# Eight merge-gate tiles of the latent branch moved from attention fillers into the 2x2 block products, with a new fill rate for the latent attention

## The chip, the core and the metric

The kernel runs on one core of one Trainium2 chip. A core has TensorE (PE) for matmuls, which writes only to PSUM, VectorE (DVE), ScalarE (ACT) and GpSimd (POOL) for elementwise work, and SyncE (SP), which issues the transfers here. Each engine works through its own instructions in their written order; semaphores make it wait for the others. The metric is the device time of one execution in microseconds (us).

## The reference

One layer of a bidirectional encoder, sequence 1024, width 1024, all in float32. `h` is the normalised input; one combined projection gives the inputs of two attentions, two SiLU gates `z` and two sigmoid merge gates `g`.

```python
h = rmsnorm(x, attn_norm_g)
(c_q, c_kv, k_rope, z_mla, q_dil, k_dil, v_dil, z_dil,
 g_mla, g_dil) = jnp.split(h @ w_in, split_points, axis=-1)
a_out = mla_attention(c_q, c_kv, k_rope, ...)      # 8 heads, 1024 x 1024 scores each
y_mla = (a_out * jax.nn.silu(z_mla)) @ w_o_mla
d_out = dilated_mixture(q_dil, k_dil, v_dil, positions)   # 24 heads, dilations 1, 4, 16
y_dil = (d_out * jax.nn.silu(z_dil)) @ w_o_dil
gate_mla = jax.nn.sigmoid(g_mla + b_gate[:D_MODEL])
gate_dil = jax.nn.sigmoid(g_dil + b_gate[D_MODEL:])
return x + (gate_mla * y_mla + gate_dil * y_dil) @ w_out   # then a final rmsnorm
```

`g_mla` is 1024 channels wide: eight tiles of 128 channels. These eight tiles are what the change is about.

## The kernel before

Every product is made from float32 pairs: an operand is split into a high part (a copy on ScalarE) and a low part (a subtraction on VectorE or POOL), and three matmuls high x high, high x low, low x high are added up (`mm3`, lines 77 to 79; `split`, lines 83 and 84). One such step on 512 columns is three matmuls; a projection tile of 128 channels by 512 tokens has eight steps, so a whole tile of 1024 tokens has 16 steps or 48 matmuls.

The stages follow each other in the program: the latent inputs and the dilated values (to about 228 us of the trace); the **block stage**; the **dilated attention**; the **latent attention**; the **end** (output gates and the last projection).

In the block stage (`blocks`, `block_steps`) the queries and keys of the dilated attention are computed by a 2x2 block scheme with seven products in place of eight: an item is two weight tiles and both token halves, seven products of four steps, 84 matmuls where two plain tiles have 96. There are twelve items. The results lie in four PSUM tiles a, b, c, d (`st_a` and so on); VectorE and ScalarE add them up, rotate them, and the result goes through the tiles `dq_st` to DRAM (`s_dq`, `s_dk`). POOL makes four block differences and seven low parts per item.

All other tiles of the combined projection that are needed late are **fillers**: the generator `fillers` walks through the list `ZG`, one step at a time, and the attentions call `feed(n)` at fixed places; `feed` adds up fractions and takes one step for each whole one. After the list the generator loads the eight pieces of the dilated branch (line 599, `zg_z` and `zg_t`, two buffers each, result in `brd_h`, `brd_l`), goes through 64 steps of the projection `w_o_dil` and then 48 of `w_o_mla` (three of its four parts; the fourth needs the last heads and stays for the end). What of these 48 steps is left when the latent attention ends is computed in the stage `output`.

In the dilated attention the order is written out by hand, fillers included. Its last pair is finished by `combine`: the softmax statistics are transposed (line 1083), sent through DRAM (`s_sd`, `c_sn`), made into factors on VectorE (lines 1098 to 1121), sent through DRAM again (`s_rr`, `bc`), and multiplied in (line 1134). In the latent attention a scheduler sets the order; a filler step is tied to the scores or transposes before it. A unit there is two query blocks of 128 rows of one head: scores `s_mla`, row maxima (line 740), exponentials `p` (line 743), transposes `pt` in four groups through two PSUM buffers (line 754), their split, and value products `av` (lines 762, 763).

Of the kernel before, what the change touches and what calls it, by code (L numbers as in the profile page):

```python
# [10 lines left out]
F32 = mybir.dt.float32  # L11
F32R = mybir.dt.float32r
I32 = mybir.dt.int32
AF = mybir.ActivationFunctionType
ALU = mybir.AluOpType
# [14 lines left out]

FIRST_FEED = 19
DIL_FEED = (1.43, 1.43, 2.5, 2)
FEED = (0.95, 0.95)

NB_BC = 5
NB_A = 6
# [3 lines left out]
T_ZM, T_QK = 0, 24  # L40

LEAD = 5

ZG = (4, 5, 6, 7, 0, 1, 2, 3, *range(16, 24), *range(8, 16))


def run_all(gen):
# [7 lines left out]
class Net:  # L55
# [393 lines left out]
    def block_steps(self, n, item, ps, tp):  # L449

        nc = self.nc
        v, act = nc.vector, nc.scalar
        a, b, c, d = (ps[x] for x in "abcd")
# [6 lines left out]
        def both():  # L460
# [9 lines left out]
            7: [lambda: add(c, 2)],  # L470
            9: [lambda: add(d, 2)],
        }
        _, g, quad, which = item
        parts = 2 if g < 2 else 1
        dst = (self.dq if which == 0 else self.dk)[g][4 * quad:4 * quad + 4]
# [59 lines left out]
                    elif half:  # L535
                        self.dma(dst[j, i, :, 0], st[i, 0][x])

        put = lambda k, f: steps.setdefault(k, []).append(f)
        r0, r1 = rope(0, b, c), rope(1, d, a)
        put(7, r0[0])  # L540
        put(8, r0[1])
# [168 lines left out]
    def mla_attention(self, ap, pp):  # L710
        nc = self.nc
        v = nc.vector
        for pair in range(4):
# [3 lines left out]
            for hh in range(2):  # L717
# [10 lines left out]
                for u in range(4):  # L728
# [3 lines left out]
                    for b2 in range(2):  # L732
                        qb = u * 2 + b2
                        qs = slice(128 * qb, 128 * qb + 128)

                        s = self.sp2.tile([128, S], F32, name="s_mla")
                        for kb in range(2):
                            ks = slice(512 * kb, 512 * kb + 512)
                            self.anchor = self.mm3(s[:, ks], q[:, 0, qs], q[:, 1, qs], k[:, 0, ks], k[:, 1, ks], True, True)
                        v.tensor_reduce(out=nm[:, hh, qb:qb + 1], in_=s, axis=AX.X, op=ALU.max, negate=True)  # L740
                        self.feed(FEED[0])
                        p = self.p_first.pop() if self.p_first else self.bp.tile([128, S], F32, name="p", bufs=3)
                        nc.scalar.activation(out=p, in_=s, func=AF.Exp, bias=nm[:, hh, qb:qb + 1], accum_out=den[:, hh, qb:qb + 1])  # L743
                        P.append(p)
# [3 lines left out]
                    for cp in range(4):  # L748
                        pt = pp.tile([128, 512], F32, name="pt", bufs=NB_PT)
                        for c2 in range(2):  # L750
                            for b2 in range(2):
                                kc = cp * 2 + c2
                                o = c2 * 256 + b2 * 128
                                self.anchor = nc.tensor.transpose(pt[:, o:o + 128], P[b2][:, 128 * kc:128 * kc + 128], self.ident)  # L754
                        self.feed(FEED[1])
                        ph = ap.tile([128, 512], F32R, name="pt_h", bufs=2)
                        pl = ap.tile([128, 512], F32R, name="pt_l", bufs=2)
                        self.split(pt, ph, pl, v)
                        for c2 in range(2):
                            kc = cp * 2 + c2  # L760
                            s = slice(c2 * 256, c2 * 256 + 256)
                            nc.tensor.matmul(a_out, vv[:, kc], ph[:, s], start=kc == 0, stop=False)  # L762
                            nc.tensor.matmul(a_out, vv[:, kc], pl[:, s], start=False, stop=kc == 7)  # L763
# [468 lines left out]
    def run(self):  # L1232
        tc, nc = self.tc, self.nc
        with ExitStack() as ctx:
# [24 lines left out]
            with tc.tile_pool(name="wpx", reuse_waits="tile", bufs=2, side="right") as self.wpx, tc.tile_pool(name="cosd", reuse_waits="tile", bufs=1, side="right") as dpool, ExitStack() as sums:  # L1259
# [34 lines left out]
                        for p in range(2):  # L1294
                            self.dma(self.dk[0][:, :, :, p, r:r + 64].rearrange("h c x t -> (c x) h t"), z[:64])
                with tc.tile_pool(name="dt", reuse_waits="tile", bufs=1, side="right") as tp, tc.tile_pool(name="st", reuse_waits="tile", bufs=1, space=PSUM) as pp:
                    self.blocks([(T_QK + (g * 2 + quad) * 4 + which * 2, g, quad, which) for quad in range(2) for g in range(3) for which in range(2)], tp, pp)
            at = ExitStack()
            pp = ctx.enter_context(tc.tile_pool(name="at", reuse_waits="tile", bufs=1, space=PSUM))
            self.dil_done, self.mla_done, self.brm, self.early, self.stop = False, 0, None, [], False  # L1300
# [98 lines left out]
```

## Time and profile before

| | |
|---|---|
| three timed runs | 1281.53, 1284.01 (median), 1286.01 us |
| the profiled execution | span 1288.1 us; no other time is given for it, so the span stands for it |
| busy, whole span | PE 1236.5, DVE 752.6, ACT 609.2, POOL 506.7 us |
| chain that ended last | PE 69%, DMA 10%, issue 4%, DVE 3% |
| transfers | 219.43 MB, mean 170 GB/s |

How to read it: a matmul's row lasts longer than its share of TensorE, since one matmul begins while the one before still drains; what one costs is the distance from start to start. The share of busy time is a mean over stages that are limited by different things, so the prediction goes by stages. In rows of the timeline the numbers are start and duration in us, and in brackets the time that the engine stood idle before the row, with what ended it.

### The profile page before, as it was taken

What the parts mean: (1) busy time and instruction counts of PE and PEld (TensorE: products, weight loads), DVE (VectorE), ACT (ScalarE), POOL (GpSimd) and SP (SyncE); (2) the same over time, 40 slices, a digit from 0 to 9 for tenths busy, and PEclk for the clock granted to TensorE, in tenths of its full rate; (3) what the DMA queues carried; (4) which work ended last, traced back from release to release, by engine and by line L of the source; (5) the groups of instructions that cost most, each with busy time, mean ns of one, the idle gap of its engine ahead of it and who ended that gap; (6) DMA issues with size and microseconds to landing.
All of it is one profiled execution on the core that took longest, in us unless ns stands there. A gap on an engine that the chain in (4) does not pass through costs nothing.

```text
span 1288.1 us, 19688 instructions
## 1 busy us (share of the span) xinstructions
PE 1236.5 (96%) x6957; PEld 1073.3 (83%) x6957; DVE 752.6 (58%) x1368; ACT 609.2 (47%) x1276; POOL 506.7 (39%) x402
## 2 busy tenths in 40 slices
PE   8979999899999999999998999999999999998998
PEld 8978999788888877888887888888888888885786
DVE  7483524466556644566565664555566666668632
ACT  6523336344444326555464552455555555554322
POOL 2342218877767715435323041311211211247522
PEclk9989999999999998999998999999999999998999
DMA  9946674276456685988879797445346535135441
GB/s 328 251 157 251 237 286 143 85 181 160 129 140 155 146 218 153 212 197 221 207 202 235 185 229 190 155 118 134 127 115 172 143 97 150 58 107 184 159 148 49
DMA packets 134482, 219.43 MB, mean 170 GB/s; under 512 B 37160, under 2 KB 66672, under 8 KB 130480
## 3 DMA queue, kind: packets, MB, share of 16 engines
q1 hardware_dynamic: 134384, 218.17, 60.2%
q8 instruction: 55, 0.90, 0.3%
q14 instruction: 43, 0.35, 0.1%
HBM read 149.37 MB, written 68.75 MB: 169 GB/s over the span
## 4 chain that ended last, share of the span: by engine, by line
PE 69%; DMA 10%; issue 4%; DVE 3%; POOL 2%; SPq 2%; ACT 1%; DVEq 0%; POOLq 0%; ACTq 0%
PE pj L77 10%; PE pj L78 10%; PE pj L79 10%; PE pt L754 4%; PE av L763 2%; DMA op_a<-s_dk 2%; PE s_mla L77 2%; PE s_mla L79 2%; PE av L762 2%; PE s_mla L78 2%; DMA bc<-s_rr 2%; PE st_a L77 2%; PE st_a L79 2%; PE st_a L78 2%; PE st_c L79 2%
## 5 line engine op out<-in xcount | busy, mean ns | idle before, releaser
L84 POOL TENSOR_TENSOR w_l<-w_raw,w_h 128x512 fp32r<-128x512 f32 (+1 forms) x176 | 227.0, 1303 | 416.8 <-ACT w_h L83 360.2
L77 PE MATMUL pj<-hT_h,w_h 128*128 128x512 f32 x384 | 156.3, 407 | 0.0
L79 PE MATMUL pj<-hT_h,w_l 128*128 128x512 f32 x384 | 152.1, 396 | 0.0
L78 PE MATMUL pj<-hT_l,w_h 128*128 128x512 f32 x384 | 152.0, 396 | 0.0
L83 ACT CAST w_h<-w_raw 128x512 fp32r<-128x512 f32 (+1 forms) x176 | 104.3, 615 | 82.3 <-POOL w_raw L427 70.4
L84 DVE TENSOR_TENSOR pt_l<-pt,pt_h 128x512 fp32r<-128x512 f32 x128 | 88.0, 688 | 66.9 <-ACT pt_h L83 66.0
L83 ACT CAST pt_h<-pt 128x512 fp32r<-128x512 f32 x128 | 74.7, 585 | 79.7 <-PE pt L754 47.7
L77 PE MATMUL pj<-w_h,hT_h 128*128 128x256 f32 x384 | 109.2, 284 | 0.0
L78 PE MATMUL pj<-w_l,hT_h 128*128 128x256 f32 x384 | 109.0, 284 | 0.0
L79 PE MATMUL pj<-w_h,hT_l 128*128 128x256 f32 x384 | 108.9, 283 | 0.0
L740 DVE TENSOR_REDUCE m_nm<-s_mla 128x1 f32<-128x1024 f32 x64 | 78.2, 1222 | 27.0 <-PE s_mla L79 26.3
L870 DVE CUSTOM_DVE_ANT_0 p<-s_ps,masks 128x256 f32<-128x256 f32 x128 | 48.8, 419 | 73.6 <-PE s_ps L861 63.9
L877 ACT ACTIVATE p<-p,d_st 128x256 f32<-128x256 f32 x128 | 64.1, 502 | 54.3 <-DVE d_st L870 54.2
L79 PEld LDWEIGHTS pj<-hT_h,w_l 128*128 128x128 f32 x384 | 72.9, 190 | 15.8
L77 PEld LDWEIGHTS pj<-hT_h,w_h 128*128 128x128 f32 x384 | 73.4, 191 | 11.2
L78 PEld LDWEIGHTS pj<-hT_l,w_h 128*128 128x128 f32 x384 | 73.2, 191 | 11.3
L743 ACT ACTIVATE p<-s_mla,m_nm 128x1024 f32<-128x1024 f32 x64 | 71.8, 1122 | 18.6 <-PE pt L754 17.6
L754 PE MATMUL pt<-consts,p 128*128 128x128 f32 x512 | 78.1, 272 | 1.3 <-ACT p L743 1.3
L77 PEld LDWEIGHTS pj<-w_h,hT_h 128*128 128x128 f32 x384 | 73.7, 192 | 0.9
L78 PEld LDWEIGHTS pj<-w_l,hT_h 128*128 128x128 f32 x384 | 73.6, 192 | 0.8
L79 PEld LDWEIGHTS pj<-w_h,hT_l 128*128 128x128 f32 x384 | 73.7, 192 | 0.8
L762 PE MATMUL av<-pt_h,op_c 128*128 128x256 f32 x256 | 68.8, 289 | 0.0
(307 smaller groups left out, 3320.0 us busy)
## 6 DMA issues: line engine op xcount, KB each, us to landing
w_raw<-wt SPq DMA_DIRECT2D x48, 512.0 KB, 3.7
op_b<-s_dq SPq DMA_DIRECT2D x32, 512.0 KB, 8.4
gate<-s_gt SPq DMA_DIRECT2D x43, 256.0 KB, 2.9
s_dq<-dq_st SPq DMA_DIRECT2D x80, 128.0 KB, 2.4
s_dk<-dq_st SPq DMA_DIRECT2D x80, 128.0 KB, 2.4
s_dv<-dv_st SPq DMA_DIRECT2D x32, 256.0 KB, 4.1
s_gt<-zg_t SPq DMA_DIRECT2D x32, 256.0 KB, 3.7
w_raw<-wv SPq DMA_DIRECT2D x12, 512.0 KB, 3.6
```

The source lines that it names most:

```text
L77: mm(out, lh, rh, start=start, stop=False, skip_group_check=skip)
L78: mm(out, lh, rl, start=False, stop=False, skip_group_check=skip)
L79: return mm(out, ll, rh, start=False, stop=stop, skip_group_check=skip)
L83: self.nc.scalar.copy(out=h, in_=raw)
L84: sub.tensor_tensor(out=l, in0=raw, in1=h.bitcast(F32), op=ALU.subtract)
L740: v.tensor_reduce(out=nm[:, hh, qb:qb + 1], in_=s, axis=AX.X, op=ALU.max, negate=True)
L743: nc.scalar.activation(out=p, in_=s, func=AF.Exp, bias=nm[:, hh, qb:qb + 1], accum_out=den[:, hh, qb:qb + 1])
L754: self.anchor = nc.tensor.transpose(pt[:, o:o + 128], P[b2][:, 128 * kc:128 * kc + 128], self.ident)
L762: nc.tensor.matmul(a_out, vv[:, kc], ph[:, s], start=kc == 0, stop=False)
L763: nc.tensor.matmul(a_out, vv[:, kc], pl[:, s], start=False, stop=kc == 7)
L870: nc.vector.tensor_tensor_reduce(out=p[:, c], in0=x["s"][:, c], in1=mask, op0=ALU.add, op1=ALU.min, scale=-0.125, scalar=3e38, accum_out=s ...
L877: nc.scalar.activation(out=p, in_=p, func=AF.Exp, scale=-1.0, bias=nm, accum_out=den)
```

## The change

The eight tiles of `g_mla` (8 to 15 in the list of tiles) leave `ZG` and become four more items of the block stage, behind the twelve of queries and keys. For them `block_steps` does not rotate: each of the four results is multiplied by the token factors `R` in PSUM, goes through a tanh on ScalarE into a `dq_st` tile, and is stored to `s_gt`. The fill rate of the latent attention, 0.95 steps at each of its 192 feeds, becomes 0.58 in the first three pairs of heads and 1.05 in the fourth. The rates of the dilated attention stay as they are.

```diff
-FEED = (0.95, 0.95)
+FEED = (0.58, 0.58, 0.58, 1.05)
-ZG = (4, 5, 6, 7, 0, 1, 2, 3, *range(16, 24), *range(8, 16))
+ZG = (4, 5, 6, 7, 0, 1, 2, 3, *range(16, 24))
+BLOCK_GATES = (8, 10, 12, 14)
...
+        put = lambda k, f: steps.setdefault(k, []).append(f)
+        if len(item) == 1:
+            def gate(i, half, x):
+                c = slice(512 * half, 512 * half + 512)
+                t = tp.tile([128, 512], F32, name=f"dq_st{i}{half}")
+                j = item[0] - T_ZM - 8 + i
+
+                def times():
+                    v.tensor_tensor(out=x, in0=x, in1=self.R[:, c], op=ALU.mult)
+
+                def tanh():
+                    act.activation(out=t, in_=x, func=AF.Tanh, scale=0.5, bias=self.hb[:, j:j + 1])
+                    self.dma(self.gt[j][:, c], t)
+                return times, tanh
+            for k, i, half, x in ((7, 0, 0, b), (7, 1, 1, a), (8, 1, 0, c), (10, 0, 1, d)):
+                def both_steps(k=k, i=i, half=half, x=x):
+                    times, tanh = gate(i, half, x)
+                    times()
+                    tanh()
+                put(k, both_steps)
+            return steps
...
-                        self.feed(FEED[0])
+                        self.feed(FEED[pair])
...
-                        self.feed(FEED[1])
+                        self.feed(FEED[pair])
...
-                    self.blocks([(T_QK + ... which) for quad in range(2) for g in range(3) for which in range(2)], tp, pp)
+                    self.blocks([(T_QK + ... which) for quad in range(2) for g in range(3) for which in range(2)] + [(T_ZM + i,) for i in BLOCK_GATES], tp, pp)
```

Line numbers of the changed kernel are one higher from line 45 on, and 21 or 22 higher behind the new lines. The change moves instructions at two places that matter here.

The first is the end of the dilated attention and the start of the latent one. On ScalarE, before, from the exponents of the last pair's combination (`c_w`) on:

```order
L1105 ACTIVATE c_w<-c_w 16x384
L624 ACTIVATE zg_t<-zg_z,consts 128x512
L83 CAST w_h<-w_raw 128x512 x2
L624 ACTIVATE zg_t<-zg_z,consts 128x512 x2
L83 CAST w_h<-w_raw 128x512 x2
L624 ACTIVATE zg_t<-zg_z,consts 128x512
L743 ACTIVATE p,m_den<-s_mla,m_nm 128x1024 x2
L83 CAST pt_h<-pt 128x512
```

and after the change:

```order
L1126 ACTIVATE c_w<-c_w 16x384
L645 ACTIVATE zg_t<-zg_z,consts 128x512
L84 CAST brd_h<-zg_z 128x512
L764 ACTIVATE p,m_den<-s_mla,m_nm 128x1024 x2
L84 CAST brd_h<-zg_z 128x512 x2
L764 ACTIVATE p,m_den<-s_mla,m_nm 128x1024
L84 CAST pt_h<-pt 128x512 x2
```

The gate fillers (`zg_t`) have gone from there, and the copies of the dilated pieces (`brd_h`) have moved ahead of the latent exponentials and between them. On VectorE at the same place, before:

```order
L617 TENSOR_TENSOR zg_z<-pj,R 128x512
L1134 TENSOR_TENSOR num<-num,bc 128x512 x2
L617 TENSOR_TENSOR zg_z<-pj,R 128x512
L740 TENSOR_REDUCE m_nm<-s_mla 128x1 x3
L84 TENSOR_TENSOR pt_l<-pt,pt_h 128x512 x2
```

and after, from the second statistics row on, with the six products of the combination (`num`) and the pieces behind them (line 620, line 599 before):

```order
L1121 TENSOR_TENSOR c_w<-c_w,c_sn 16x128
L761 TENSOR_REDUCE m_nm<-s_mla 128x1
L1121 TENSOR_TENSOR c_w<-c_w,c_sn 16x128
L1123 TENSOR_TENSOR c_w<-c_w,c_sn 16x128 x3
L1133 TENSOR_TENSOR c_d<-c_w,c_sn 16x128 x3
L1134 TENSOR_TENSOR c_d<-c_d 16x128
L1135 TENSOR_TENSOR c_d<-c_d 16x128
L1139 TENSOR_SCALAR c_d<-c_d 16x128
L1140 RECIPROCAL c_d<-c_d 16x128
L1142 TENSOR_TENSOR c_w<-c_w,c_d 16x128 x3
L1155 TENSOR_TENSOR num<-num,bc 128x512 x6
L638 TENSOR_TENSOR zg_z<-pj,R 128x512
```

Two row maxima have moved up into the combination; behind the last row shown come three pieces and only then the third row maximum. On TensorE 12 scores stand behind the last 12 fillers of the dilated attention, then one matmul that reads `brd_h`, then the first transposes `pt`.

The second place is the start of the dilated attention, on the queue of SP. Before, where the first two heads' operands (`op_a`, `op_b`, `op_c`) are loaded:

```order
L73 DMA s_dq_64<-dq_st_4645 32x1024 x4
L73 DMA op_b<-s_dq_62 64x2048 x2
L73 DMA op_a<-s_dk_65 64x1152 x2
L73 DMA op_c<-s_dv_68 128x9x128
L73 DMA op_b<-s_dq_62 64x2048 x2
L73 DMA op_a<-s_dk_65 64x1152 x2
L73 DMA op_c<-s_dv_68 128x9x128
L73 DMA w_raw<-wt 128x1024
L73 DMA s_dk_67<-dq_st_4743 32x1024 x4
L73 DMA s_dk_67<-dq_st_4744 32x1024 x4
```

and after:

```order
L74 DMA op_b<-s_dq_62 64x2048 x2
L74 DMA op_a<-s_dk_65 64x1152 x2
L74 DMA s_gt<-dq_st_5356 128x512
L74 DMA s_gt<-dq_st_5360 128x512
L74 DMA s_gt<-dq_st_5364 128x512
L74 DMA op_c<-s_dv_68 128x9x128
L74 DMA op_b<-s_dq_62 64x2048
L74 DMA s_gt<-dq_st_5369 128x512
L74 DMA op_b<-s_dq_62 64x2048
L74 DMA op_a<-s_dk_65 64x1152 x2
L74 DMA op_c<-s_dv_68 128x9x128
L74 DMA w_raw<-wt 128x1024
```

The eight stores of the last key item, which stood behind all these loads, have moved up by four items; the four stores of the last gate item stand among the loads.

More of the change, by code (lines that the diff above doesn't have):

```diff
@@ L536, in store @@
                         self.dma(dst[j, i, :, 0], st[i, 0][x])
-        put = lambda k, f: steps.setdefault(k, []).append(f)
         r0, r1 = rope(0, b, c), rope(1, d, a)
@@ L1296, in run @@
                 with tc.tile_pool(name="dt", reuse_waits="tile", bufs=1, side="right") as tp, tc.tile_pool(name="st", reuse_waits="tile", bufs=1, space=PSUM) as pp:
-                    self.blocks([(T_QK + (g * 2 + quad) * 4 + which * 2, g, quad, which) for quad in range(2) for g in range(3) for which in range(2)], tp, pp)
+                    self.blocks([(T_QK + (g * 2 + quad) * 4 + which * 2, g, quad, which) for quad in range(2) for g in range(3) for which in range(2)] + [(T_ZM + i,) for i in BLOCK_GATES], tp, pp)
             at = ExitStack()
```

## The prediction

> **What bounds the kernel now.** I read the busy time by stage first, cut where the trace changes its work: block products, dilated attention, latent attention, end.
>
> ```profile
> core 0: us, PE busy (x) PEld busy (x) DVE busy (x) ACT busy (x) POOL busy (x), PEclk, DMA share, GB/s
> 228.00:460.00 232.00, 231.28 (x994) 187.66 (x995) 143.01 (x226) 93.53 (x181) 169.63 (x132) 0.99 0.56 144
> 460.00:818.00 358.00, 339.97 (x1996) 297.70 (x1995) 206.50 (x525) 180.82 (x458) 122.00 (x108) 0.98 0.82 204
> 818.00:1156.00 338.00, 335.56 (x1958) 290.18 (x1957) 211.23 (x277) 182.29 (x329) 71.80 (x58) 1.00 0.43 124
> 1156.00:1288.00 132.00, 119.45 (x518) 94.63 (x517) 72.21 (x120) 43.28 (x90) 58.72 (x41) 0.97 0.39 132
> ```
>
> After the length of a stretch, the first number is TensorE's. It fills the block stage and the latent attention; in the dilated attention it misses 18 us and at the end 13. So work taken from it pays in the two full stages, and only if no other engine's chain then comes to light.
>
> By the order of issue, 512-column matmuls move like this: blocks +336; the stretch between the last dilated work and the first latent scores 132 to 12; fillers inside the latent attention 555 to 336; output stage 501 to 456. Net -48.
>
> **Blocks, four items more.**
>
> ```profile
> L77 PE MATMUL st_a<-s_h,w_h x48: 392/392/392, 241.5 to 457.2; 128*128 128x512 f32 x48
> ```
>
> These are four per item, so the first and last start lie eleven items and three steps (of three matmuls, 0.7 us each) apart: (215.7 - 2.1) / 11 = 19.42 us an item. Four more cost 77.7 us. Nothing else bounds them: POOL has 170 of 232 us and the same 11 instructions for each item; VectorE has 143 and nine instructions per gate item where rotation and splits needed 17 to 21.
>
> **Latent attention, 219 matmuls fewer.**
>
> ```profile
> 883.00 0.40 PE L77 MATMUL pj<-hT_h,w_h 128*128 128x512 f32 x1
> ...
> 885.08 0.28 PE L762 MATMUL av<-pt_h,op_c 128*128 128x256 f32 x1
> ```
>
> Nine fillers start in 2.08 us, 0.231 each. 219 of them are 50.6 us, if the rest of the stage keeps TensorE full.
>
> **The hole between the attentions.** Here I expect the change to lose its profit.
>
> ```profile
> 788.12 0.27 PE L1083 MATMUL pt<-consts,d_st 128*96 128x128 f32 x1
> 788.15 0.47 PE L77 MATMUL pj<-hT_h,w_h 128*128 128x512 f32 x1
> ...
> 818.20 0.40 PE L77 MATMUL s_mla<-op_b,op_a 96*128 96x512 f32 x1
> ```
>
> From the last dilated work on TensorE (788.1) to the first latent scores pass 30.1 us, all 132 of those fillers. What else happens in them is the last pair's combination:
>
> ```profile
> 788.81 0.83 SPq L73 DMA_DIRECT2D s_sd<-av_t  x1
> 793.06 1.28 SPq L73 DMA_DIRECT2D c_sn<-s_sd  x3
> 797.31 0.20 DVE L1098 COPY c_w<-c_sn 16x128 f32<-16x128 f32 x1
> 805.74 0.32 SPq L73 DMA_DIRECT2D s_rr<-c_w  x1
> 807.35 7.48 SPq L73 DMA_DIRECT2D bc<-s_rr  x12
> 818.12 1.04 DVE L1134 TENSOR_TENSOR num<-num,bc 128x512 f32<-128x512 f32 x1 [0.87 <-DMA bc<-s_rr]
> 821.04 1.12 ACT L743 ACTIVATE p<-s_mla,m_nm 128x1024 f32<-128x1024 f32 x1 [0.52 <-DVE m_nm L740]
> ```
>
> The chain is two DMA round trips, small VectorE work, twelve loads issued one after another, and the products, which end at 788.1 + 30.6. Afterwards 12 fillers and 12 scores are left: 24 x 0.23 = 5.6 us. Then TensorE's next row reads brd_h, and ScalarE has that copy ahead of the first latent exponential (its order is shown above). The copy needs the product of piece 0, which VectorE has behind the six products by the last loads. Without the fillers' multiplications VectorE saves about 2 us of that chain; two row maxima now inside it cost 2 x 1.22. So products end again near +30.6; then 0.6 (last filler's multiplication), 0.7 (piece 0) and 0.6 (copy), and the exponential starts at about +32.0, against +32.9 above: **-0.9 us**. The 120 fillers (27.3 us) were free cover; TensorE stands still for some 26 us. Bounds: -3 (DMA in less traffic) and +2 (a late piece).
>
> **New waits in the latent attention.** All eight pieces are now issued at once, through two buffers:
>
> ```profile
> gate<-s_gt SPq DMA_DIRECT2D x43, 256.0 KB, 2.9
> 869.10 0.62 ACT L83 CAST brd_h<-zg_z 128x512 fp32r<-128x512 f32 x1 [1.25 <-DVE zg_z L599]
> L84 POOL TENSOR_TENSOR brd_l<-zg_z,brd_h x8: 1266/1286/1292, 838.5 to 946.9; 128x512 fp32r<-128x512 f32 x8
> ```
>
> A buffer goes through load 2.9 (as for a gate of that size), product 0.7, copy 0.6, POOL 1.3: 5.5 us for two pieces, so the eighth comes some 20 us after the first. VectorE and ScalarE have them in line between row maxima, exponentials and splits. Followed row by row, the third unit of two query blocks starts about 4 us late; with the cold clock (below) I take 6.
>
> Then the fillers end: five or six units in pair 2 have none and the next few have one or two steps, some eight units in all.
>
> ```profile
> 873.40 0.28 PE L763 MATMUL av<-pt_l,op_c 128*128 128x256 f32 x1
> 873.52 0.60 PE L754 MATMUL pt<-consts,p 128*128 128x128 f32 x4
> 873.87 0.48 PE L77 MATMUL pj<-hT_h,w_h 128*128 128x512 f32 x1
> L743 ACT ACTIVATE p<-s_mla,m_nm 128x1024 f32<-128x1024 f32 x64 | 71.8, 1122 | 18.6 <-PE pt L754 17.6
> L83 ACT CAST pt_h<-pt 128x512 fp32r<-128x512 f32 x128 | 74.7, 585 | 79.7 <-PE pt L754 47.7
> L84 DVE TENSOR_TENSOR pt_l<-pt,pt_h 128x512 fp32r<-128x512 f32 x128 | 88.0, 688 | 66.9 <-ACT pt_h L83 66.0
> ```
>
> A bare unit costs TensorE 12 scores x 0.23, four groups of transposes at 0.44 (0.35 and a slower matmul behind), 16 value products x 0.12: 6.4 us. If everything in it were in line, it would be 4 x (0.36 + 0.59 + 0.69 + 0.47) + 1.3 for one exponential = 9.7. With two buffers of transposes the halves overlap, so I stay near the lower end: 0.6 us a unit, 5 us for eight (bounds 0 and 26). The burst of six pieces at pair 3 gets 2 (0 to 6), as it is shorter and behind full fillers. Together **+13** (4 to 25).
>
> **End, 45 matmuls fewer.**
>
> ```profile
> 1159.00:1192.00 33.00, 26.81 (x96) 18.84 (x94) 29.63 (x34) 14.12 (x25) 24.76 (x17) 0.90 0.56 183
> 1165.60 2.48 DVE L1184 SCALAR_TENSOR_TENSOR gate<-gate,pj 128x512 f32<-128x512 f32 x4 [1.74 <-PE pj L79]
> 1186.17 0.68 DVE L84 TENSOR_TENSOR mg_l<-gate,m 128x512 fp32r<-128x512 f32 x1
> 1186.77 1.78 DVE L84 TENSOR_TENSOR wout_l<-wo_raw,wout_h 128x512 fp32r<-128x512 f32 x1
> 1192.17 0.48 PE L77 MATMUL pj<-wout_h,m 128*128 128x512 f32 x1 [2.01 <-ACT wout_h L83]
> ```
>
> Between the last value product and the first output product VectorE is busy 29.6 of 33 us, so TensorE's 45 x 0.231 = 10.4 us are mostly cover. From 1165.6 VectorE runs 29 instructions up to that product, 0.92 us each. It can begin some 3 us earlier now, as no four-step units wait for a last weight tile, and by the order has about 25 ahead of the first output product: together 6 us; a TensorE that comes in cold gives 2 back. **-4** (-10 to +1).
>
> The Trainium skill's page "SBUF — State Buffer" (section Who interferes with whom) says that a VectorE instruction with two SBUF inputs and a GpSimd one that reads SBUF exclude each other. The 1.78 beside 0.68 for like shapes agrees; by it fewer matmuls bring nothing here, 0 instead of -4.
>
> **Start of the dilated attention.** This is the real gain.
>
> ```profile
> 473.08 9.18 SPq L73 DMA_DIRECT2D s_dk<-dq_st  x8
> 484.79 0.42 DVE L870 CUSTOM_DVE_ANT_0 p<-s_ps,masks 128x256 f32<-128x256 f32 x1 [9.59 <-DMA s_dk<-dq_st]
> 485.92 1.18 PE L884 MATMUL pt<-consts,p 128*128 128x128 f32 x4 [4.97 <-ACT p L877]
> 487.75 0.63 PE L77 MATMUL pj<-hT_h,w_h 128*128 128x512 f32 x1
> ...
> 491.59 0.68 PE L884 MATMUL pt<-consts,p 128*128 128x128 f32 x4
> 486.00:492.00 6.00, 6.00 (x21) 4.82 (x22) 2.33 (x8) 4.47 (x14) 5.44 (x5) 0.52 0.39 131
> ```
>
> The last key block's eight stores stand behind ten loads, and the first probabilities take over their buffers. After the change four gate stores take their place, three of them ahead of most loads; the keys left 78 us earlier. The 5.0 us wait goes, and with it six us at a granted clock of 0.52 (nine fillers in 3.84 us, not 2.08), 2.9 us: **-7.9** (-9 to -2, if the gate stores are late among the loads).
>
> The same row prices the cold clock: a 5 us wait costs 2.9 us. The hole of 26 us will cost at most as much, within the 6 above. The Trainium skill's page "TensorE: Matmul & The Clock Gate" (Part 1: The HAM clock gate) gives half rate until one window of about 3.4 us was busy; by that the price is an estimated 1.7 us and the sum 1 us lower. It speaks against thinning fillers only where a wait is as long as a window; the waits of bare units are not.
>
> **Sum.** 77.7 - 50.6 - 0.9 + 13 - 4 - 7.9 = **+27.3 us**. The profiled execution has a span of 1288.1, 4.1 over the median of the runs, 1284.0; carrying the difference over, 1284.0 + 27.3 = 1311.3.
>
> **Rivals.**
> 1. The hole closes: first exponentials run when the first scores are there, near +7, not +32. That takes 25 us, and the 6 of the start, off the sum: 1280, faster. It decides from about 27 us saved on. For it: the scores need nothing of the combination. Against it: two in-order engines have a piece ahead. Chance 0.07, of which 0.05 faster, 0.02 the same.
> 2. The latent attention starves: bare units cost the full 9.7 us, 21 us more than taken: 1332. For it: ScalarE waits 48 us for transposes even now. Against it: TensorE waits only for 2 us of that stage today. Chance 0.11.
> 3. The cover is not needed: the end gains all 10.4 and the latent attention loses 6 instead of 13: 1298. Chance 0.12.
> 4. The forecast, 1302 to 1320: 0.70.
>
> The range leaves out rival 1 and most of 2: 1298 to 1325. Faster by more than 0.3% (3.9 us, about what a measurement of this kernel tells from no change) 0.05, within it 0.03, slower 0.92.
>
> **What would show it.** The block stage is 78 us longer; no wait of 5 us at the first L905 transposes; TensorE idle for about 26 us before the first pt of the latent attention, with ScalarE's brd_h as the last to come; a granted clock near 0.5 behind it; the latent attention shorter by 35 to 45 us; the stretch from its end to the first output product 27 to 33 us. I am wrong if the idle time before that pt is under 10 us, or if bare units run in under 6.5 or over 9 us.

## The result, and the profile after

The changed kernel takes 1324.95 us (median of six runs, 1320.42 to 1328.62), the kernel before, timed beside it, 1283.15 (six runs, 1276.74 to 1287.33): a ratio of 1.0329, 95% interval 1.0302 to 1.0357, 41.8 us slower. The forecast was 27.3 us more. The direction was right, the size was some 14 us too small (1.0329 times the prediction's 1284.0 is 1326.3, beyond the range's 1325; the plain median lies just at that bound).

The profiled execution of the changed kernel has a span of 1318.6 us. Busy time by stage, in the columns of the prediction's first fence, cut within 2 us of the block stage's start, the first filler, the last statistics of the dilated attention, the first and the last latent exponential, and the first output product:

```profile
core 0: us, PE busy (x) PEld busy (x) DVE busy (x) ACT busy (x) POOL busy (x), PEclk, DMA share, GB/s
222.90:532.20 309.30, 309.30 (x1340) 251.12 (x1339) 172.84 (x273) 128.21 (x243) 224.70 (x176) 1.00 0.53 139
532.20:852.20 320.00, 304.95 (x1849) 268.87 (x1848) 186.79 (x487) 170.87 (x439) 112.89 (x101) 0.98 0.85 211
852.20:882.50 30.30, 5.79 (x27) 4.45 (x26) 15.04 (x27) 2.66 (x6) 7.08 (x6) 0.62 0.48 147
882.50:1181.50 299.00, 285.00 (x1673) 245.70 (x1674) 196.60 (x257) 163.86 (x299) 56.25 (x46) 0.98 0.41 112
1181.50:1222.40 40.90, 27.83 (x117) 20.11 (x116) 35.33 (x43) 17.23 (x30) 25.92 (x18) 0.83 0.52 161
```

In the third row TensorE works for 5.8 of 30.3 us: the hole has lost its fillers and kept its length. In the fourth it is idle for 14 us of a stage that was full before. The hole in the timelines of TensorE, ScalarE and VectorE:

```profile
857.61 0.39 PE L80 MATMUL s_mla<-op_b,op_a 96*128 96x512 f32 x1
882.63 0.80 PE L78 MATMUL pj<-brd_h,w_h 128*128 128x512 f32 x1 [24.64 <-ACT brd_h L84]
...
881.96 0.62 ACT L84 CAST brd_h<-zg_z 128x512 fp32r<-128x512 f32 x1 [0.96 <-DVE zg_z L620]
882.49 1.11 ACT L764 ACTIVATE p<-s_mla,m_nm 128x1024 f32<-128x1024 f32 x1
...
858.42 0.21 DVE L1119 COPY c_w<-c_sn 16x128 f32<-16x128 f32 x1 [4.96 <-DMA c_sn<-s_sd]
...
878.26 1.33 DVE L1155 TENSOR_TENSOR num<-num,bc 128x512 f32<-128x512 f32 x1 [0.56 <-DMA bc<-s_rr]
879.51 0.68 DVE L638 TENSOR_TENSOR zg_z<-pj,R 128x512 f32<-128x512 f32 x1
881.24 0.69 DVE L620 TENSOR_TENSOR zg_z<-zg_z,zg_t 128x512 f32<-128x512 f32 x1 [1.04 <-DMA zg_t<-s_zs]
```

TensorE stands 24.6 us, and brd_h is the last to come, ahead of the first exponential, as forecast (some 26 us). The start of the last pair of heads looks different from the forecast. TensorE, VectorE and SP's queue there:

```profile
1099.03 0.60 PE L775 MATMUL pt<-consts,p 128*128 128x128 f32 x4
...
1101.20 0.36 PE L783 MATMUL av<-pt_h,op_c 128*128 128x256 f32 x1
1105.29 0.58 PE L784 MATMUL av<-pt_l,op_c 128*128 128x256 f32 x1 [3.72 <-DVE pt_l L85]
...
1106.10 1.05 PE L775 MATMUL pt<-consts,p 128*128 128x128 f32 x4
...
1109.18 0.27 PE L775 MATMUL pt<-consts,p 128*128 128x128 f32 x1
...
1097.93 1.23 DVE L761 TENSOR_REDUCE m_nm<-s_mla 128x1 f32<-128x1024 f32 x1 [0.55 <-PE s_mla L80]
1103.94 0.69 DVE L620 TENSOR_TENSOR br_x<-br_x,gate 128x512 f32<-128x512 f32 x1 [4.79 <-DMA br_x<-s_ma]
1104.55 0.68 DVE L85 TENSOR_TENSOR pt_l<-pt,pt_h 128x512 fp32r<-128x512 f32 x1
...
1094.23 0.34 SPq L74 DMA_DIRECT2D s_ma<-num  x1
1101.12 0.34 SPq L74 DMA_DIRECT2D br_x<-s_ma  x1
```

This is one unit, between its first transposes and the next unit's: 10.15 us without a filler. The piece of the latent branch goes out to DRAM at 1094.23 (`s_ma`), its load follows 6.9 us later and lands 2.8 us after that; its product stands in VectorE's line in between, and the low half `pt_l`, for which TensorE waits, stands behind it. I call this a **stall at a piece**.

To compare kernels I count for each unit what it takes beyond 0.231 us per filler and 6.45 us for twelve scores, sixteen transposes and sixteen value products (the value at which most units of before stand; 0.233 for each score and 0.119 for each value product more or fewer). The sum over the units, without the last two, which run into the end, is the last column (not counted for e7, where useless steps stand among the units); the other columns are the lengths of the stages, cut as above, with everything behind the last exponential as "rest". One run of e4, 1380.6 us at a granted clock of 0.87 where the others have 0.97, is left out of its ratio.

| kernel | ratio to before (95%) | up to the blocks | blocks | dilated | hole | latent | rest | units too long by |
|---|---|---|---|---|---|---|---|---|
| before | 1 | 228.7 | 234.7 | 324.7 | 32.9 | 326.5 | 140.5 | 5 |
| after | 1.0329 (1.0302 to 1.0357) | 221.6 | 310.8 | 319.8 | 30.3 | 299.0 | 137.2 | 27 |
| e1 | 1.0284 (1.0260 to 1.0308) | 222.6 | 312.4 | 318.2 | 31.5 | 294.2 | 138.6 | 23 |
| e2 | 1.0380 (1.0343 to 1.0418) | 220.1 | 310.8 | 323.6 | 30.4 | 299.7 | 138.8 | 28 |
| e3 | 1.0339 (1.0315 to 1.0362) | 223.3 | 311.1 | 306.5 | 35.9 | 305.8 | 138.5 | 34 |
| e4 | 1.0387 (1.0363 to 1.0411) | 220.1 | 311.2 | 317.2 | 31.6 | 307.7 | 138.8 | 36 |
| e5, one item | 1.0110 (1.0083 to 1.0137) | 219.4 | 255.5 | 318.5 | 32.9 | 326.1 | 138.6 | 22 |
| e6, two items | 1.0038 (1.0017 to 1.0060) | 223.4 | 272.0 | 317.3 | 34.8 | 302.6 | 138.0 | 22 |
| e7 | 1.0365 (1.0332 to 1.0398) | 223.1 | 310.9 | 318.2 | 32.2 | 302.7 | 138.6 | |
| e8, three items | 1.0176 (1.0151 to 1.0201) | 221.5 | 293.1 | 317.0 | 38.6 | 297.5 | 137.1 | 26 |
| e9, one item | 1.0077 (1.0046 to 1.0107) | 224.1 | 255.5 | 315.3 | 32.9 | 320.9 | 139.9 | 22 |
| e10, two items | 0.9998 (0.9977 to 1.0019) | 224.0 | 273.5 | 316.4 | 33.7 | 295.0 | 143.3 | 21 |
| e11, four items | 1.0247 (1.0217 to 1.0278) | 222.8 | 310.9 | 313.8 | 29.7 | 293.1 | 137.3 | 23 |
| e12, two items | 0.9969 (0.9949 to 0.9988) | 223.0 | 272.3 | 318.0 | 33.4 | 292.2 | 139.5 | 11 |
| e13, one item | 0.9953 (0.9934 to 0.9972) | 219.5 | 255.5 | 319.6 | 32.9 | 306.6 | 141.4 | 6 |
| e14, no item | 0.9972 (0.9952 to 0.9992) | 221.6 | 233.9 | 326.0 | 32.9 | 325.3 | 140.4 | 4 |
| e15, four items | 1.0198 (1.0174 to 1.0222) | 220.0 | 312.4 | 316.1 | 11.2 | 308.0 | 137.6 | 38 |

The first column matters for reading the two profiles against each other. The kernels do not differ up to the blocks, and the 16 other profiles have 219.4 to 224.1 us there; only the profiled execution of before has 228.7. Some 7 us of its 1288.1 belong to that execution, so the spans differ by only 30.5, the stages behind by 37.6, the medians by 41.8.

### The profile page after: what moved, and what is told of

Read it like the earlier page. It is cut to its first block, busy times and chain, and to the rows that moved or that the text cites. A ratio compares the mean times of both kernels' runs of the same rounds, so it can differ in the third digit from the quotient of the medians.

```text
span 1318.6 us, 19690 instructions
## 1 busy us (share of the span) xinstructions
PE 1233.6 (94%) x6909; PEld 1067.8 (81%) x6909; DVE 766.6 (58%) x1393; ACT 621.3 (47%) x1298; POOL 544.7 (41%) x433
## 4 chain that ended last, share of the span: by engine, by line
PE 68%; DMA 14%; DVE 7%; issue 4%; POOL 3%; ACT 2%; SPq 2%; DVEq 0%; ACTq 0%; POOLq 0%
PE pj L78 9%; PE pj L79 9%; PE pj L80 9%; PE pt L775 4%; PE st_c L80 2%; PE st_c L79 2%; PE st_c L78 2%; PE st_d L79 2%; PE st_d L80 2%; PE st_a L80 2%; PE st_d L78 2%; PE st_a L78 2%; PE st_a L79 2%; SPq L74 2%; DMA bc<-s_rr 2%
## 5 line engine op out<-in xcount | busy, mean ns | idle before, releaser
L85 POOL TENSOR_TENSOR w_l<-w_raw,w_h 128x512 fp32r<-128x512 f32 (+1 forms) x186 | 239.9, 1302 | 392.9 <-ACT w_h L84 336.8
L84 ACT CAST w_h<-w_raw 128x512 fp32r<-128x512 f32 (+1 forms) x186 | 111.2, 616 | 114.4 <-POOL w_raw L428 91.7
L78 PE MATMUL pj<-hT_h,w_h 128*128 128x512 f32 x256 | 102.1, 399 | 0.0
L80 PE MATMUL pj<-hT_h,w_l 128*128 128x512 f32 x256 | 101.9, 398 | 0.0
L79 PE MATMUL pj<-hT_l,w_h 128*128 128x512 f32 x256 | 101.9, 398 | 0.0
L428 POOL TENSOR_TENSOR w_raw<-w_raw 128x512 f32<-128x512 f32 x64 | 83.7, 1308 | 0.0
L775 PE MATMUL pt<-consts,p 128*128 128x128 f32 x512 | 80.9, 280 | 2.2 <-ACT p L764 2.0
L784 PE MATMUL av<-pt_l,op_c 128*128 128x256 f32 x256 | 68.8, 293 | 8.9 <-DVE pt_l L85 8.9
L783 PE MATMUL av<-pt_h,op_c 128*128 128x256 f32 x256 | 71.5, 300 | 0.9 <-DVE num L833 0.9
L775 PEld LDWEIGHTS pt<-consts,p 128*128 128x128 f32 x512 | 61.5, 143 | 7.7 <-ACT p L764 4.1
```

Source lines behind the costliest of these rows:

```text
L78: mm(out, lh, rh, start=start, stop=False, skip_group_check=skip)
L79: mm(out, lh, rl, start=False, stop=False, skip_group_check=skip)
L80: return mm(out, ll, rh, start=False, stop=stop, skip_group_check=skip)
L84: self.nc.scalar.copy(out=h, in_=raw)
L85: sub.tensor_tensor(out=l, in0=raw, in1=h.bitcast(F32), op=ALU.subtract)
L428: self.nc.gpsimd.tensor_tensor(out=b[out], in0=b[x], in1=b[y], op=ALU.subtract)
```

## The experiments

The ratios are against runs of before on the same chip beside them; the stage lengths come from one profile each.

### The stall at the last pair (e1)

The pieces of the third pair are held back until the last pair has four row maxima, and the rate of the last pair is raised so that the latent attention holds as many fillers as in the changed kernel (units count from 0; the last pair's are 24 to 31):

```diff
-            while todo[0][0] >= self.mla_done:
+            while todo[0][0] >= self.mla_done or todo[0][0] == 2 and self.maxima < 52:
                 yield
             j, h2 = todo.pop(0)
-            self.piece(...)
+            with tc.issue_after(self.row_max.ins):
+                self.piece(...)
-FEED = (0.58, 0.58, 0.58, 1.05)
+FEED = (0.58, 0.58, 0.58, 1.2)
```

> The changed kernel, with the first of the two pieces of the third pair of heads put about seven VectorE rows later (behind the fifth row maximum of the last pair), so that its loads have landed when VectorE comes to it. If the loss of some 9 us around the start of the last pair is VectorE standing in its line before that product (4.8 us, and the cold clock behind TensorE's wait of 3.7 us), 4 to 7 us are gained over the changed kernel, and the wait of 3.7 us is gone. If the loss comes from the units without fillers, which this edit makes one or two more, the time stays within 2 us of the changed kernel or gets longer by up to 3.

VectorE and SP's queue of this run:

```profile
1109.15 1.23 DVE L763 TENSOR_REDUCE m_nm<-s_mla 128x1 f32<-128x1024 f32 x1 [0.83 <-PE s_mla L80]
1110.29 0.68 DVE L620 TENSOR_TENSOR br_x<-br_x,gate 128x512 f32<-128x512 f32 x1
...
1097.39 0.34 SPq L74 DMA_DIRECT2D s_ma<-num  x1
1104.29 0.34 SPq L74 DMA_DIRECT2D br_x<-s_ma  x1
```

The round trip is the same (6.9 us to the load), the product no longer waits for it. Unit 23 took 5.26 us, not 10.15, the latent attention 4.8 less, and the ratio fell by 0.45 points, 6 us (the two intervals just meet). The account of the stall holds at this place.

### The start of the dilated attention (e2)

The list of items begins with the four gate items, so that a key item is last again.

> The changed kernel with its four gate items ahead of the twelve items of queries and keys, so that a key item is last again. If the gain at the start of the dilated attention comes from the last item of the block stage, the wait for the late key stores is back: about 4 us of wait and 3 us of cold clock in the first 40 us of that stage, 5 to 8 us slower than the changed kernel. If that gain has another cause, no difference (within 2 us).

TensorE's row at that start:

```profile
553.65 1.18 PE L905 MATMUL pt<-consts,p 128*128 128x128 f32 x4 [5.26 <-ACT p L898]
```

The wait is back (5.0 in before, 0.9 in the changed kernel), and the stage is 3.8 us longer. The ratio rose by 0.5 points, but the intervals overlap, so the time alone would not show it; the wait does: the gain comes from the last item. Measured from the first filler, the 16th group of four transposes came 6.5 us earlier in the changed kernel than in before, the end of the stage 4.9. Half way through the stage both kernels wait for an operand load; first the changed kernel's row, then that of before:

```profile
686.59 0.55 PE L881 MATMUL s_ps<-op_a,op_b 128*128 128x256 f32 x1 [4.83 <-DMA op_a<-s_dk]
```

```profile
622.59 0.35 PE L860 MATMUL s_ps<-op_a,op_b 128*128 128x256 f32 x1 [3.04 <-DMA op_a<-s_dk]
```

The lead falls there from 6.7 to 2.3 us, and part of it comes back later. The longer wait was followed by a granted clock of 0.50 (687 to 690), the shorter one by the full clock. In the other profiles this wait differs too, so no run shows that the earlier start lengthened it.

### The hole (e3, e8, e7, e11, e15)

e3 thins the fillers of the dilated attention so that 123 are left for the hole.

```diff
-DIL_FEED = (1.43, 1.43, 2.5, 2)
+DIL_FEED = (1.2, 1.2, 2.1, 2)
```

> The changed kernel with lower fill rates in the first parts of the dilated attention, so that 123 filler matmuls instead of 12 are left for the stretch between the attentions; what is computed and the latent attention's fillers are the same. If TensorE sets the length of the dilated attention, its stage gets shorter by up to 111 x 0.231 = 25.6 us (15 to 26), the stretch between the attentions keeps its 30 us but with TensorE busy, and with the cold clock gone too the kernel is 15 to 29 us faster than the changed kernel. If the dilated attention is set by its transfers and its own chain, TensorE's idle time only moves there, and the time is that of the changed kernel within 4 us.

Neither: the dilated attention got shorter by 13.3 of the 25.6 us, so by this run TensorE sets about half of it; the hole took 5.6 of them back and the latent attention 6.8. With gate tiles in the hole again, the row maxima and exponentials stand behind those tiles' products, and TensorE waited 6.2 us for the first exponential. The total did not move.

e8 puts the last of the four items back among the fillers and changes nothing else.

```diff
-ZG = (4, 5, 6, 7, 0, 1, 2, 3, *range(16, 24))
-BLOCK_GATES = (8, 10, 12, 14)
+ZG = (4, 5, 6, 7, 0, 1, 2, 3, *range(16, 24), 14, 15)
+BLOCK_GATES = (8, 10, 12)
```

> The changed kernel with three gate items in place of four, and the last two tiles as fillers again: they come to stand between the attentions (108 fillers there in place of 12); everything behind is as in the changed kernel. If that stretch has its length from the combination of the last pair and not from TensorE, the 96 matmuls are free there: 19.4 us less than the changed kernel for the item, and 0 to 4 more for the warm clock, so 19 to 24 us faster than it (ratio to before about 1.014 to 1.018). If they push the combination and the first latent units back, as in the run with thinner rates in the dilated attention, only 8 to 16 us.

20 us less by the ratios: the price of the item and a little more, so the 96 matmuls cost nothing that the timed runs show. The profiles differ by 13.9 only, 17.7 less in the blocks and 8.3 more in the hole; how much of those 8.3 belongs to that one execution stays open. Behind the fillers TensorE still waits:

```profile
870.33 0.79 PE L78 MATMUL pj<-brd_h,w_h 128*128 128x512 f32 x1 [11.18 <-ACT brd_h L84]
```

So the hole was free cover for most of them, and the last item bought nothing.

e7 fills the hole with work that nobody reads, to price the clock alone.

```diff
                 while not self.dil_done:
+                    if self.manual:
+                        ps = self.pj.tile([128, 512], F32, name="pj")
+                        self.mm3(ps, *self.at(w, 0), self.hTh[:, 0, 0:512], self.hTl[:, 0, 0:512], True, True)
                     yield
```

> The changed kernel with 35 useless filler steps (105 matmuls whose result nobody reads) between the first latent scores and the first transposes, so that TensorE is busy for some 24 of the 25 us in which it stood still. If the cold clock behind that wait is a part of the loss at the start of the latent attention, the first 20 us run at full clock and 3 to 5 us are gained over the changed kernel. If that start is set by the pieces' loads alone, through which VectorE goes in its order, no difference (within 1.5 us). In neither case do 105 more matmuls cost anything.

The granted clock by stretches, of this run (first two rows) and of the changed kernel (last two):

```profile
882.00:892.00 10.00, 9.59 (x36) 7.71 (x37) 3.74 (x5) 4.38 (x8) 3.75 (x3) 0.83 0.63 210
892.00:902.00 10.00, 10.00 (x54) 8.31 (x53) 6.66 (x8) 6.02 (x12) 3.85 (x3) 1.00 0.49 162
```

```profile
882.00:892.00 10.00, 8.47 (x24) 6.19 (x24) 3.08 (x3) 4.65 (x8) 3.61 (x3) 0.59 0.75 247
892.00:902.00 10.00, 7.96 (x39) 7.10 (x40) 7.25 (x9) 6.34 (x13) 2.76 (x3) 0.83 0.49 144
```

The clock was nearly full and nothing was gained (1.0365 against 1.0329, the intervals overlap); some of the useless steps ran behind the first transposes, so the run cannot exclude that a small gain was paid out for them. VectorE's third row maximum stood behind pieces as before: the pieces' loads set the start, not the clock.

e11 gives all pieces a distance from their loads and lets the first one wait for a row maximum; e15 is e11 and also drains the last gate tile's multiplication and tanh as soon as the fillers run out (the second cut shows e15 against e11).

```diff
+        self.waiting.append((max(self.maxima + 2, due), product))
...
+    def products(self, rest=False):
+        while self.waiting and (rest or self.maxima >= self.waiting[0][0]):
+            with self.tc.issue_after(self.row_max.ins):
+                self.waiting.pop(0)[1]()
```

```diff
                 while not self.dil_done or len(self.waiting) == 2 or not self.maxima:
+                    if self.manual:
+                        next(self.tail, None)
                     yield
```

> The same edit with all four gate items and the changed kernel's rates; the first piece now also stands behind the first row maximum, so that ScalarE has no piece ahead of the first latent exponential, and the first five units have no fillers. If the hole before the first transposes was held open by the piece in line, TensorE begins 10 to 20 us earlier and the waits of the start and of the last pair go: 15 to 30 us faster than the changed kernel (ratio to before 1.009 to 1.021). If the combination itself holds VectorE, only the waits go and the bare units at the start cost 4 us: 2 to 8 us faster than the changed kernel (ratio 1.026 to 1.031).

> The run with four items and late pieces, with one edit more: the multiplication and tanh of the last gate tile are issued as soon as the fillers have run out, not behind the last combination. In that run ScalarE had this tanh, behind VectorE's six products, ahead of the first latent exponential and stood 17.5 us at it. Now the first two exponentials can run some 14 us after the last statistics, not 29.7. If these lines alone keep the hole open (the first rival of the prediction), TensorE goes on from there: 10 to 16 us faster than the run before. If VectorE's six products keep it open all the same, since the first low halves and the third row maximum stand behind them in its order, only the first transposes move up: 1 to 6 us.

e11: 10 us less than the changed kernel by the ratios, between its two expectations, but the hole is as long as before (29.7). With the piece gone from ScalarE's line, that tanh stood in it:

```profile
876.56 0.72 ACT L655 ACTIVATE zg_t<-zg_z,consts 128x512 f32<-128x512 f32 x1 [17.48 <-DVE zg_z L648]
```

e15: 6 us less again (the intervals just meet). ScalarE, VectorE and TensorE of e15:

```profile
859.69 1.09 ACT L784 ACTIVATE p<-s_mla,m_nm 128x1024 f32<-128x1024 f32 x1
...
876.38 1.11 ACT L784 ACTIVATE p<-s_mla,m_nm 128x1024 f32<-128x1024 f32 x1 [10.30 <-DVE m_nm L780]
...
873.37 1.84 DVE L1175 TENSOR_TENSOR num<-num,bc 128x512 f32<-128x512 f32 x2 [0.47 <-DMA bc<-s_rr]
875.13 1.22 DVE L780 TENSOR_REDUCE m_nm<-s_mla 128x1 f32<-128x1024 f32 x1
...
877.64 0.79 PE L80 MATMUL s_mla<-op_b,op_a 96*128 96x512 f32 x1 [10.11 <-ACT p L784]
```

The first exponentials came 18.5 us earlier behind the last statistics than in e11 (hole 11.2), but behind the first transposes TensorE waited 10.1 us: the third row maximum stands behind VectorE's six products, which wait for the combination's loads. So three places in in-order lines held the hole, one behind the other: ScalarE's piece, ScalarE's tanh, and VectorE's products of the combination. The third is read from this trace; no run moved it.

### Thin fillers or stalls (e4, e5, e6, e9, e10, e12, e13, e14)

e4 only spreads the fillers: FEED 0.49 in place of 0.58 in the first three pairs.

> The changed kernel with a fill rate of 0.49 in place of 0.58 in the first three pairs of heads, so that the same fillers reach to the end of the third pair and no long run of units is left without one. If a unit without fillers costs 1.1 us more than one with some (7.6 against 6.45 us net of its fillers), 4 to 7 us are gained. If what is lost depends on the number of fillers alone and not on where they stand, no difference (within 2 us).

Slower by 0.6 points. The long bare stretch was gone, but a stall came up at the end of the second pair, where there was none:

```profile
1025.06 1.23 DVE L761 TENSOR_REDUCE m_nm<-s_mla 128x1 f32<-128x1024 f32 x1 [0.54 <-PE s_mla L80]
1031.66 0.69 DVE L620 TENSOR_TENSOR br_x<-br_x,gate 128x512 f32<-128x512 f32 x1 [5.38 <-DMA br_x<-s_ma]
```

With 9 fillers and fewer, units 17 to 22 were still 5 us too long, where the changed kernel's were 7.5. Bare units are thus not the main loss. e5 and e6 are doses of the change with the hole full (rates 0.82 and 0.66); e6 has (8, 10), and the tiles left out are fillers behind range(16, 24).

```diff
-BLOCK_GATES = (8, 10, 12, 14)
+BLOCK_GATES = (8,)
```

> The changed kernel with one gate item in the block stage in place of four; the other six gate tiles are fillers again, so that the stretch between the attentions has its 132 fillers back, and the latent rate is 0.82 throughout (477 fillers in the latent attention, 75 behind it; before 555 and 93). By the account of stages, against before: one item 19.4 more, 78 latent fillers x 0.231 = 18.0 less, some 6 less at the start of the dilated attention, nothing at the end: 4 to 7 us faster than before (ratio 0.9945 to 0.997). If thinner fillers cost the latent attention as they do in the changed kernel even while the stretch before it is full, 0 to 10 us slower than before.

> The same with two gate items; 132 fillers between the attentions, 363 inside the latent one, 93 behind it, rate 0.66 throughout. By the account against before: 38.8 more, 192 x 0.231 = 44.4 less, some 6 less at the start of the dilated attention, and losses of thin units, 10 units with 9 fillers or fewer at 0.5 to 1.1 us and one wait of about 5 us for a piece of the latent branch: 10 to 16 us. Together between 2 us faster and 5 us slower than before (ratio 0.998 to 1.004). If the lost latent fillers cost nothing by themselves, 10 to 12 us faster.

One item cost 14 us where 4 to 7 were to be gained, more than two items (5 us). The block stage and the dilated attention did as said; the latent attention, with 78 fillers fewer, was as long as before. In e5 16 of the 22 us are in units 11, 15, 23 and 24 (5.9, 5.7, 2.1 and 2.4 us too long), with no unit bare. VectorE's waits for the loads of pieces, in e5 (total, times, longest) and then in before:

```profile
DVE br_x L620 <- DMA br_x<-s_ma: 5.7, 2, 4.5
DVE br_x L620 <- DMA gate<-s_zs: 5.5, 2, 3.8
DVE zg_z L620 <- DMA zg_t<-s_zs: 4.6, 2, 2.9
```

```profile
DVE zg_z L599 <- DMA zg_t<-s_zs: 9.1, 4, 4.8
DVE br_x L599 <- DMA gate<-s_zs: 4.8, 5, 1.8
DVE br_x L599 <- DMA br_x<-s_ma: 1.2, 1, 1.2
```

VectorE stood nearly as long in before, 15.1 against 15.8 us, but there it cost TensorE little (units 5 us too long). I take it that not the wait's length counts but whether low halves stand behind it that TensorE needs before its fillers run out.

e9 and e10 have the distance of two row maxima shown above with one and two items, at the rates of e5 and e6.

> One gate item as in the run with one item (rate 0.82), but each piece's product is put two row maxima or more behind the issue of its loads, and for pieces of the latent branch not ahead of the fifth row maximum of the next pair. 132 fillers between the attentions, 450 inside the latent one, 102 behind it. If the 14 us that one item cost came from VectorE standing at pieces that were still being loaded (units 11, 15, 22, 23 and 24 were 17 us too long together), those go: against before 20 for the item, 6 less at the start of the dilated attention, 105 x 0.231 = 24 less in the latent attention, 0 to 2 more behind it and 0 to 5 for thin units: 3 to 10 us faster than before (ratio 0.992 to 0.998). If thin fillers cost by themselves, it stays 8 to 15 us slower than before.

> The same edit with two gate items, rate 0.66; 336 fillers inside the latent attention, 120 behind it. The run with two items and early products was 0.4% slower than before, with some 17 us too many in units 6 to 8 and 22 to 25. If VectorE's place in line is their cause, 8 to 15 of those go, less up to 6 for 27 more fillers behind the attention: 2 to 10 us faster than before (ratio 0.992 to 0.998). If not, ratio 1.002 to 1.008.

Half a success. In e10 units 22 to 25 were 2 us too long in place of e6's 9, but units 6 to 8 were 13 in place of 10, two of them bare, and in e9 the stalls of units 11 and 15 stayed. Rows of SP's queue and of VectorE in e10 say why:

```profile
913.11 0.42 SPq L76 DMA_DIRECT2D zg_t<-s_zs  x1
...
915.42 0.69 DVE L624 TENSOR_TENSOR zg_z<-zg_z,zg_t 128x512 f32<-128x512 f32 x1 [3.43 <-DMA zg_t<-s_zs]
```

The load itself was issued 2.3 us ahead of the product, when VectorE stood at it already. The edit had put the product later, not the load: the pieces have only two buffers, shared with the gate tiles. e12 (two items), e13 (one) and e14 (none, the rates of before) give the pieces the five `bc` buffers, take one at a step of the remaining gate tiles, and keep three row maxima of distance. e12 and e13 also have rates of their own (372 and 468 fillers in the latent attention, where e10 and e5 have 336 and 477).

```diff
-    def piece(self, src, j, half, zj, br, x, z):
+    def piece(self, src, j, half, zj, br, due=0):
+        x, z = (self.ap.tile([128, 512], F32, name="bc", bufs=NB_BC) for _ in range(2))
...
+        self.waiting.append((max(self.maxima + 3, due), product))
...
                         if kc < 7:
+                            if self.dil_done and todo and self.maxima and len(self.waiting) < 2:
+                                j, h2 = todo.pop(0)
+                                self.piece(self.da, j, h2, 4 + j, self.brd)
                             yield
```

> Two gate items; the pieces of both branches use the five bc buffers, one is taken at a step of the remaining gate tiles instead of at each half tile, and each product stands three row maxima or more behind its loads; rates 0.58, 0.58, 0.58, 1.0. 132 fillers between the attentions, 372 inside the latent one, 84 behind it, and one unit with less than 6. If all that two items lose lies in VectorE's stand at pieces and in units without fillers, units 6 to 8 keep to 6.5 us net of fillers (13 us too long in the run before), and against before: 38 more for the items, 6 less at the start of the dilated attention, 183 x 0.231 = 42 less in the latent attention, up to 4 for thin units: 6 to 10 us faster than before (ratio 0.992 to 0.996). If units with 9 to 12 fillers are slower by themselves, the ratio is 0.998 to 1.004.

> The same edit with one gate item and rates 0.82, 0.80, 0.78, 0.95: 132 fillers between the attentions, 468 inside the latent one, 84 behind it. By the same account 20 more for the item, 6 less at the start of the dilated attention, 87 x 0.231 = 20 less in the latent one: 4 to 8 us faster than before (ratio 0.994 to 0.997). If the stalls of units 11, 15 and 23 are not due to the place of the products, they stay, and the ratio is 1.005 to 1.010.

> The kernel before with the same edit of the pieces and no gate item in the block stage; rates and fillers are those of before (132, 555, 93). Units 3, 6 and 7 of before were together some 4 us too long. If it is the pieces' place alone that helps in the runs with one and two items, this one gains as much, 2 to 4 us at most (ratio 0.997 to 0.999), and less than the run with two items. If the edit does nothing in a latent attention that is full, the ratio is 1.000 within 0.002.

e12 lies between its two expectations: the stalls are gone, and no unit is more than 1.8 us too long, 11 us in all; what causes these was not tested. VectorE's waits for pieces in e13 are one row:

```profile
DVE bc L625 <- DMA bc<-s_zs: 0.9, 1, 0.9
```

e13 fell from 1.0110 (e5) to 0.9953, 20 us with one item in both, of which some 2 are its nine fewer latent fillers: the stalls were the loss. It beats both kernels, by 0.5% the kernel before (0.9934 to 0.9972). But e14, with no item at all, has 0.9972 (0.9952 to 0.9992): the better place and the buffers of the pieces bring as much alone, and what the item adds lies within the measurement. (In the profiles only 1.0 of e14's 3.6 us against before stands behind the start of the blocks, so by stages its gain is not shown.) By stages e13 against e14 has blocks +21.6, dilated attention -6.4, latent attention -18.7, rest +1.0.

## Why the prediction was too small

**Blocks, +77.7: right.** 310.8 - 234.7 = 76.1.

**The hole, -0.9, and free cover: right.** The stage got 2.6 shorter, TensorE idle in 24.6 of it; e8 confirms that the last item's matmuls were free there. The way there was a little different: in before the products end at +31.0 by their row, not +30.6, and in the changed kernel at +27.4, as the first round trip's data were there 3 us sooner; the wait of 1.0 for piece 0's load gave that much back. Both lie within the bounds given, but that they partly offset each other is luck. Taking first the piece and then the tanh out of ScalarE's line (e11, e15) brought 10 and 6 us, not the first rival's 25: by e15's trace VectorE's products hold TensorE then.

**Start of the dilated attention, -7.9: right in kind, 3 too large.** The wait went as forecast, 6.5 us were there at the 16th group, and 4.9 were left at the stage's end, behind the longer operand wait shown above.

**End, -4: right.** The rest is 3.3 shorter; from the last value product to the first output product pass 30.2 us, before 33.1, and VectorE is busy 35.3 of the 40.9 us ahead of that output product.

**Latent attention, -50.6 and +13: here it failed.** The stage fell by 27.5, not 37.6, and outside the 35 to 45 named as a sign. The fillers were worth their 0.231; the new waits were sized too low. Units 0 to 3 are 8.5 too long (6 taken). Units 17 to 22 are 7.5 too long (5 taken); four bare ones in a row are read directly:

```profile
1057.02 0.60 PE L775 MATMUL pt<-consts,p 128*128 128x128 f32 x4
...
1087.40 0.27 PE L775 MATMUL pt<-consts,p 128*128 128x128 f32 x1
```

30.4 us for units 18 to 21, 7.6 each, forecast 7.0 (the second rival's 1332 lies near the measured time, but needs 9.7 each). Units 23 to 25 are 8.8 too long, and that is the step: "The burst of six pieces at pair 3 gets 2 (0 to 6), as it is shorter and behind full fillers". There is no such burst, and no filler there: the last pair's fillers wait for the third pair's two pieces, the first a round trip of 9.7 us through DRAM, and VectorE stands at it. The only chain that the prediction has for a piece is load, product, copy and POOL's difference, without the store ahead of the load. Another 3 us lie in single units; 5 us that before lost in its own units were not credited.

Of the 10 us missed in the latent attention, the stall at the last pair is 7, the start and the bare units 2.5 each, the single units 3, less the 5 of before. e1 removed the stall at the last pair; the start and the bare units are read from the trace alone. The rest of the distance to 41.8 is the dilated attention's 3 and some 4 us by which the profiled execution of the changed kernel lies under its median, less some 3 by which the blocks and the hole came out shorter.

By the Trainium skill's page "TensorE: Matmul & The Clock Gate" (Part 1, on the engines' queues) VectorE and ScalarE take their instructions strictly in order. The rows above agree: `pt_l` at 1104.55 stands behind the piece that waited 4.79 us, and in e15 the third row maximum behind six products.

## What to carry to other kernels

Fillers that lay in a chain of DMA round trips cost nothing here, and taking them out brought nothing; count what each filler covers before it is made cheaper. An operation that waits for a DRAM round trip must stand in its engine's line behind as much other work as the trip is long, and its loads need buffers of their own; here the scheduler put it too early, and a change of the filler rate alone brought such a stall up at a new place (e4). Try a change at several doses, and its repair without the change: here the measurement cannot tell the repair alone from repair and change together.

## What the runs showed of the hardware

A store of 256 KB to DRAM and the load of the same data took 6.9 us from the store's issue to the load's and 2.8 more to the product where the first half of a pair was stored; SP's queue shows five operand loads of the next head ahead of it, from 1090.2 on. For a second half, with one such load 3.4 us ahead, the changed kernel has 2 us:

```profile
972.30 0.32 SPq L74 DMA_DIRECT2D s_ma<-num  x1
974.33 0.32 SPq L74 DMA_DIRECT2D br_x<-s_ma  x1
```

That the store waits behind those loads is argued from this order; no run moved them. After TensorE's wait of 24.6 us the granted clock was 0.59 over 882 to 892; behind a wait of 3.7 us the transposes at 1106.10 took 1.05 in place of 0.60. Keeping TensorE busy gave the clock back and no time (e7).
